# FFN of a hybrid decoder step: other edges between projection, row blocks and end, and split weights kept in memory

## The chip, the cores and the metric

One core of a Trainium2 chip runs the whole kernel. It has five engines with their own instruction queues, which run in order: TensorE (PE: matmuls; PEld is its load of the stationary operand), VectorE (DVE), ScalarE (ACT), GpSimd (POOL) and SyncE (SP), which here only issues DMAs. The metric is device microseconds of one execution, and the figure that is compared is a median over runs.

## The reference

The reference runs one decoder layer on 2048 prompt rows with 16 learned meta rows ahead of them, and on 8 samples of 4 rows. Two groups of heads (retention and gated DeltaNet) mix the normalised rows; then come an output projection, a residual with a layer norm, a SwiGLU feed-forward network and a second residual with a layer norm. The change touches what follows the mixers:

```python
hp = layer_norm(ALPHA * hp + mp, ln1_g[layer], ln1_b[layer])
...
def swiglu(h, w_gate_up, w_down):
    gu = h @ w_gate_up
    return (jax.nn.silu(gu[..., :D_FF]) * gu[..., D_FF:]) @ w_down
...
hp = layer_norm(ALPHA * hp + swiglu(hp, w_gate_up[layer], w_down[layer]), ln2_g[layer], ln2_b[layer])
```

The width is 1024 and D_FF is 2816, so the hidden width is 22 slices of 128. All is float32.

## The kernel before

The kernel has three stages: `attention`, `project` (output projection, first norm) and `ffn`. A framework places the semaphores and chooses each engine's order of instructions: it works through the program text by priority, earliest text first, with its own model of durations, so that later text fills what it takes for gaps. On the chip each engine then keeps that order. Memory is taken in pools that open and close like a stack; a tile in a new pool waits until what lay at its address is released.

**Precision.** A float32 operand is split into a high part (a cast on ACT, L311) and a low part (a subtraction on DVE or POOL, L318); a product is three matmuls (high by high, high by low, low by high), issued by `mm3` at L368. All matmuls of a product with 4 pieces of K make 12 matmuls.

**Projection.** `project` takes 17 tiles: 16 of 128 prompt rows and one of the 32 sample rows. For a tile it multiplies the mixed heads by `wout` (48 matmuls of 512 columns into two PSUM tiles `d`), adds the residual on DVE (L1199), runs `layer_norm` (statistics on DVE, an inverse square root in some ten dependent DVE instructions of one column at L263 to L270, scaling on ACT at L302, gain on DVE at L304, bias on POOL at L306), and stores the rows. Two tiles later `transposed` turns the rows round on PE (L1209), copies them (L1210), and for each pair of tiles `sums` makes four differences on POOL (L1222) and stores seven operands in DRAM (L1229).

**FFN.** Rows are worked through in three `BLOCKS` of pairs of tiles. Gate and up for a hidden slice f are done with a scheme of seven half-size products instead of eight (`gateup`: X, Y, Z, X, Y, W, Z), so that a product streams n columns: n is 384 for the blocks with three pairs of prompt tiles, and 272 for the one with two pairs and the sample rows. In the kernel before that one comes first. The stationary operands are sums and differences of pieces of gate and up: `weights` loads a slice of `gu` (L1274, 1 MB), forms S on POOL (L1288) and splits it (ACT, DVE). It does this for every f in every block, one slice ahead. The moving operands are the seven stored ones; `tokens` loads (L1394) and splits them at the start of a block. After every second f, `down` multiplies the hidden slices by `w_down` (512 columns into PSUM tiles `d`, 6 matmuls for a tile and half), one unit of work between two products, and DVE adds each result to the rows `y` (L1380). The last `down` of a block also norms each tile and stores it. `step` calls between products place this work: `units` are pieces of `down`, `ws` the preparation of the next weights.

**At the edges.** The pools of `ffn` open after those of `project` have closed. At the end of a block the last `down` with its norms runs between the first products of the next one. After the last f of the last block the units that are left run to the end.

## Time and profile before

| | us |
|---|---|
| median of 3 runs (3038.37 to 3047.83) | 3041.84 |
| the profiled execution's own time | 3041.72 |
| its span, first to last instruction | 3039.9 |
| PE busy | 2865.1 (94%) |
| DVE busy | 2184.7 (72%) |
| ACT busy | 1148.7 (38%) |
| POOL busy | 1039.0 (34%) |

Busy PE is not PE at its peak: matmuls overlap, and one that is counted as 0.39 us long can follow the one before it by 0.23 us. The table by stretches therefore is read by the number of matmuls in a stretch, times the distance from one to the next where nothing is in the way. A chain of waits is followed back from an instruction to what released it; a line "DVE dl L318" in it says which engine and which line of the kernel the time went to.

### The profile page before, as it was taken

How to read it: one execution, taken by the hardware profiler on the slowest of the kernel's cores; microseconds unless marked ns; L12 is line 12 of the kernel's file. 1: busy time of each engine (PE TensorE's matmuls, PEld its weight loads, DVE VectorE, ACT ScalarE, POOL GpSimd, SP SyncE). 2: the span in 40 equal slices, each digit the busy share in tenths (PEclk: the TensorE clock that was granted, in tenths of full speed). 3: DMA queues.
4: the chain of work that ended last, by engine and by line, in shares of the span. 5: the costliest groups of instructions: out<-in, count | busy, mean ns of one | idle time of the engine just before them, and what ended most of it. 6: DMA issues, size and time to landing. Idle time of an engine off the chain costs nothing.

```text
span 3039.9 us, 47059 instructions
## 1 busy us (share of the span) xinstructions
PE 2865.1 (94%) x17930; PEld 2550.1 (84%) x17930; DVE 2184.7 (72%) x4547; ACT 1148.7 (38%) x2571; POOL 1039.0 (34%) x927
## 2 busy tenths in 40 slices
PE   7999999999999999999869999899999989999995
PEld 6888888888888887978758889789999988999994
DVE  7777677766776676667677777886666688666667
ACT  2434444444444435432243333433333343233331
POOL 1222222221222131236545444453343335343332
PEclk9999999999999999999979999999999999999998
DMA  7544544443444333366542222431212244121211
GB/s 272 200 172 161 182 147 156 157 151 147 156 152 153 122 114 122 111 206 205 191 167 84 91 84 97 149 124 59 77 59 74 76 136 139 56 77 62 71 63 42
DMA packets 132274, 384.75 MB, mean 127 GB/s; under 512 B 18144, under 2 KB 53520, under 8 KB 115664
## 3 DMA queue, kind: packets, MB, share of 16 engines
q1 hardware_dynamic: 132048, 381.74, 36.0%
q8 instruction: 141, 2.31, 0.3%
q14 instruction: 85, 0.70, 0.1%
HBM read 294.14 MB, written 87.56 MB: 126 GB/s over the span
## 4 chain that ended last, share of the span: by engine, by line
PE 59%; DVE 21%; issue 6%; POOL 6%; ACT 4%; DMA 3%; SPq 0%; POOLq 0%; ACTq 0%; DVEq 0%
PE pj L368 18%; PE d L368 16%; PE Y L368 4%; PE X L368 4%; POOL S L1288 4%; PE Z L368 4%; PE W L368 3%; DVE dl L318 2%; DVE s34l L318 1%; ACT s34h L311 1%; DMA fr<-bd 1%; DVE cacc L822 1%; ACT junk L773 1%; DVE y L1380 1%; DVE lnst L286 1%
## 5 line engine op out<-in xcount | busy, mean ns | idle before, releaser
L368 PE MATMUL pj<-wh,xT 128*128 128x256 f32 (+2 forms) x2176 | 458.2, 294 | 8.4 <-ACT wh L311 4.2
L368 PE MATMUL pj<-xT,wh 128*128 128x512 f32 (+1 forms) x1280 | 379.8, 381 | 1.8 <-ACT cpre L806 1.1
L368 PEld LDWEIGHTS pj<-wh,xT 128*128 128x128 f32 (+1 forms) x2176 | 352.5, 187 | 13.1 <-ACT wh L311 4.4
L368 PE MATMUL pj<-wl,xT 128*128 128x256 f32 (+3 forms) x1088 | 309.8, 285 | 0.5 <-POOL wl L318 0.5
L368 PE MATMUL d<-dl,fh 128*128 128x512 f32 (+1 forms) x748 | 299.9, 401 | 9.2 <-DVE dl L318 8.6
L368 PE MATMUL d<-dh,fh 128*128 128x512 f32 (+1 forms) x748 | 294.0, 394 | 8.1 <-DVE y L1380 8.0
L368 PE MATMUL d<-dh,fl 128*128 128x512 f32 (+1 forms) x748 | 297.6, 398 | 2.1 <-POOL fl L318 2.1
L318 POOL TENSOR_TENSOR fl<-ta,fh 128x384 fp32r<-128x384 f32 (+1 forms) x66 | 70.9, 1074 | 642.7 <-ACT fh L311 642.7
L1288 POOL TENSOR_TENSOR S<-fr 128x512 f32<-128x512 f32 x132 | 209.8, 1607 | 168.9 <-DVE s34l L318 108.3
L1380 DVE TENSOR_TENSOR y<-y,d 128x512 f32<-128x512 f32 (+1 forms) x352 | 238.8, 680 | 31.4 <-PE d L368 31.2
L368 PEld LDWEIGHTS pj<-xT,wh 128*128 128x128 f32 x1280 | 211.9, 194 | 25.2 <-issue 3.4
L368 PE MATMUL pj<-xT,wl 128*128 128x512 f32 (+1 forms) x640 | 229.6, 359 | 0.0
L368 PEld LDWEIGHTS pj<-wl,xT 128*128 128x128 f32 (+1 forms) x1088 | 204.5, 188 | 0.9 <-POOL wl L318 0.8
L368 PEld LDWEIGHTS d<-dl,fh 128*128 128x128 f32 (+1 forms) x748 | 138.0, 184 | 40.3 <-DVE dl L318 22.3
L368 PEld LDWEIGHTS d<-dh,fl 128*128 128x128 f32 (+1 forms) x748 | 138.1, 185 | 35.5 <-POOL fl L318 2.6
L318 DVE TENSOR_TENSOR a11l<-fr,a11h 128x512 fp32r<-128x512 f32 x66 | 52.3, 792 | 158.1 <-ACT a11h L311 158.1
L368 PEld LDWEIGHTS d<-dh,fh 128*128 128x128 f32 (+1 forms) x748 | 137.9, 185 | 30.7 <-DVE y L1380 11.3
L311 ACT CAST a11h<-fr 128x512 fp32r<-128x512 f32 x66 | 41.0, 621 | 291.9 <-DMA fr<-gu 291.9
L368 PE MATMUL X<-b,a11h 128*128 128x384 f32 (+1 forms) x528 | 125.5, 322 | 18.1 <-ACT b L311 13.9
L822 DVE SCALAR_TENSOR_TENSOR cacc<-cpre,cw,cacc 128x512 f32<-128x512 f32 (+1 forms) x144 | 115.8, 805 | 32.0 <-ACT cacc L820 30.5
L368 PE MATMUL Y<-t,s34h 128*128 128x384 f32 (+1 forms) x528 | 128.8, 328 | 8.5 <-DVE u L1325 4.3
L368 PEld LDWEIGHTS pj<-xT,wl 128*128 128x128 f32 x640 | 122.7, 192 | 16.8 <-issue 0.8
(333 smaller groups left out, 7809.5 us busy)
## 6 DMA issues: line engine op xcount, KB each, us to landing
fr<-gu SPq DMA_DIRECT2D x132, 512.0 KB, 3.9
wh<-parts SPq DMA_DIRECT2D x45, 1024.0 KB, 5.0
wl<-parts SPq DMA_DIRECT2D x45, 1024.0 KB, 6.7
fr<-dn SPq DMA_DIRECT2D x66, 512.0 KB, 3.9
parts<-wh SPq DMA_DIRECT2D x15, 1024.0 KB, 5.3
parts<-wl SPq DMA_DIRECT2D x15, 1024.0 KB, 6.9
raw<-wret SPq DMA_DIRECT2D x16, 512.0 KB, 5.2
raw<-wgd SPq DMA_DIRECT2D x16, 512.0 KB, 7.1
```

Source lines behind the costliest of these rows:

```text
L286: i = nc.vector.bn_stats(out=st[:, o], in_=x)
L311: i = nc.scalar.copy(out=h, in_=src)
L318: i = (nc.vector if el == "dve" else nc.gpsimd).tensor_tensor(out=l, in0=src, in1=h.bitcast(F32), op=ALU.subtract)
L368: self.nc.tensor.matmul(out, lhsT=a(k), rhs=b(k), start=first and k == 0 and i == 0, stop=last and k == kn - 1 and i == 2, skip_group_chec ...
L773: nc.scalar.activation(out=junk, in_=p[:, j, :], func=AF.Square, accum_out=sq[:, a, t:t + 1])
L822: nc.vector.scalar_tensor_tensor(out=ac, in0=pre[:, i:i + N], scalar=w(i), in1=ac, op0=ALU.mult, op1=ALU.add)
L1288: op = lambda o, x, z, f: nc.gpsimd.tensor_tensor(out=o, in0=x, in1=z, op=f)
L1380: nc.vector.tensor_tensor(out=ys, in0=ys, in1=p, op=ALU.add)
```

## The change

The block with the sample rows becomes the last one. The pools for raw loads, gate/up weights, two of the seven token operands and the rows `y`, and all PSUM pools of the FFN, open before the projection; the projection's accumulators and transposes share the three PSUM tiles `d`, and its transposed rows and differences use the FFN's row tiles. The transposes of the last two projection tiles become units between the first FFN products. In block 1 each split weight is also stored in DRAM (`keep`, 2 x 14 KB a partition and slice); blocks 2 and 3 load it from there (`kept`) and neither load `gu` nor form S nor split. Norms at a block's end run for a group of tiles, one inverse square root for the group, in steps (`chores`). The middle `down` of a block goes through all tiles for one half of the columns and then for the other. In the last slice the order of products changes (`late`), half of its `down` runs before the last product, and `finish` does the other half: six PSUM tiles, to which the rows `y` are added by a matmul with the identity, normed from PSUM.

```diff
 BLOCKS = [
-    Block([(_P(0), _P(1), 128), (_P(2), _P(3), 128), (0, NS // 2, NS // 2)]),
...
+    Block([(_P(i), _P(i + 1), 128) for i in (0, 2, 4)]),
+    Block([(_P(i), _P(i + 1), 128) for i in (6, 8, 10)]),
+    Block([(_P(12), _P(13), 128), (_P(14), _P(15), 128), (0, NS // 2, NS // 2)]),
 ]
+LAID = (("a11", 0, 4), ("s12", 4, 8), ("a12", 12, 4), ("a22", 16, 4), ("s34", 20, 8))
...
+    def layer_norms(self, work, g, b, pool, sums=None):
...
+        for i, (x, rows) in enumerate(work):
...
+                nc.vector.bn_stats(out=st[:, o], in_=sums[i][o] if sums else x[:, 512 * o:512 * o + 512])
+            nc.vector.bn_aggr(out=mv[:rows, i], in_=st)
+            yield
+        r = self.rsqrt(mv[:, :, 1], T, 128, pool, 1.0, LN_EPS)
...
+        yield
...
+            if sums and i == T - 1:
+                for o, p in zip(at, src):
+                    nc.vector.scalar_tensor_tensor(out=x[:, o], in0=p, scalar=mv[:rows, i, 0:1], in1=g[:rows, o], op0=ALU.subtract, op1=ALU.mult)
+                for o in at:
+                    nc.vector.scalar_tensor_tensor(out=x[:, o], in0=x[:, o], scalar=r[:rows, i:i + 1], in1=b[:rows, o], op0=ALU.mult, op1=ALU.add)
...
+            for o, p in zip(at, src) if sums else [(slice(0, D), x)]:
+                nc.scalar.activation(out=x[:, o], in_=p, func=AF.Identity, scale=r[:rows, i:i + 1], bias=nm[:rows, i:i + 1])
+            nc.vector.tensor_tensor(out=x, in0=x, in1=g[:rows], op=ALU.mult)
+            for u, o in enumerate(at):
+                (nc.vector if sums and u else nc.gpsimd).tensor_tensor(out=x[:, o], in0=x[:, o], in1=b[:rows, o], op=ALU.add)
+            yield
...
+        spare = lambda i: self.fy.tile([128, D], F32, tag=f"y{i}", name="spare")
...
+            x = xr[r0] = spare(int(second)).rearrange("p (a b) -> p a b", a=8)
+            for j in range(2):
+                p = self.pd.tile([128, 512], F32, tag="d", name="tr").rearrange("p (a b) -> p a b", a=4)
...
+        def rest():
+            for i in (N - 2, N - 1):
+                yield from transposed(i)
...
-            pd = self.pool("p_d", bufs=3, space=PSUM, es=s)
-            pt = self.pool("p_t", bufs=3, space=PSUM, es=s)
...
+            ap, rp, sp, yp, pg, pd = self.fa, self.fr, self.fs, self.fy, self.pg, self.pd
...
+            def kept(f, w):
+
+                yield
+                for i, (name, o, m) in enumerate(LAID):
+                    t = [ap.tile([128, m, 128], F32R, tag=name + x, name=name + x, bufs=2 if name == "a11" else 1) for x in "hl"]
+                    for x, y in zip(t, self.wd[f]):
+                        nc.sync.dma_start(out=x.bitcast(F32).rearrange("p a b -> p (a b)"), in_=y[:, 128 * o:128 * (o + m)])
+                    w.update(named(name, t))
+                    yield
+                    if i in (0, 2):
+                        yield
...
+            def keep(f, name, t):
+                o, m = next((o, m) for n, o, m in LAID if n == name)
+                for x, y in zip(t, self.wd[f]):
+                    nc.sync.dma_start(out=y[:, 128 * o:128 * (o + m)], in_=x.bitcast(F32).rearrange("p a b -> p (a b)"))
+                return named(name, t)
...
-                t = parts(pair(2), "s34")
+                w.update(keep(f, "s34", parts(pair(2), "s34")))
...
+                if late:
+
+                    product(X, "a12", "b21", more=True)
+                    step(2)
+                    product(Y, "s3", "t3", more=True)
+                    add(u3, x1, Y)
+                    step(3)
+                    product(W, "a22", "t4")
+                    add(x1, u3, W)
+                    swish(X, x1, 0, "ta")
+                    step(4)
+                    product(Z, "s1", "t1")
+                    add(z5, u3, Z)
+                    add(u2, u2, Z)
+                    step(5)
+                    late(fh, fl)
+                    X = ps("X")
+                    product(X, "s4", "b22")
+                    add(u2, u2, X)
+                    swish(u2, z5, 1, "tb")
...
+            def normed(bi, group):
+
+                tiles, y = BLOCKS[bi].tiles(), rows_of[bi]
+                yield from self.layer_norms([(y[j][:tiles[j][1]], tiles[j][1]) for j in group], g2, b2, sm)
+                for j in group:
+                    nc.sync.dma_start(out=self.O["y"][tiles[j][0]:sum(tiles[j]), :], in_=y[j][:tiles[j][1]])
+                    if bi + 1 < len(BLOCKS) and j < len(BLOCKS[bi + 1].tiles()):
+                        load_rows(bi + 1, j)
...
+                order = [(n, i) for n in range(2) for group in groups for i in group]
+                if first or last:
+                    order = [(n, i) for group in groups for i in group for n in range(2)]
...
+            def finish(bi, fs, w, fi):
...
+                banks = [(pd, "d")] * 3 + [(pg, t) for t in "YWZ"]
...
+                        down1(blk, fs, w, fi, i, n, p, False)
+                        nc.tensor.matmul(p, lhsT=self.ident[:rows, :rows], rhs=y[i][:rows, 512 * n:512 * n + 512], start=False, stop=True)
...
+                for _ in self.layer_norms([(y[j][:tiles[j][1]], tiles[j][1]) for j in group], g2, b2, sm, sums):
+                    pass
...
+                    t = (self.fb if j < 2 else bp).tile([128, 2, 4 * 384], F32R, tag=name, name=name)
...
+                        self.split(r, h[:, o:o + m], l[:, o:o + m], "act", "pool" if u and bi else "dve")
...
+            units, chores = [rest], []
...
+                    ws = iter(()) if (bi, f) == end else weights(nf, nw) if bi == 0 and nf else kept(nf, nw)
...
+                        for _ in range(3 if (bi, f) == end else 1 if f % 2 or i >= (2 if bi + f else 4) else 0):
+                            some(units)
+                        for _ in range(2 if f == 2 else 1):
+                            some(chores)
+                        next(ws, None)
...
+                with self.weights_es:
+                    self.attention()
+                    self.fr = self.pool("f_r", bufs=4, es=late, side="right")
...
+                    self.pg = self.pool("p_g", space=PSUM, es=late)
+                    rest = self.project()
+                self.ffn(rest)
```

## Rows read from the trace of the kernel before

**Rows 1.** The page's head: the span, the busy time of each engine, and what the DMA engines moved in each of 40 equal slices of the span (76 us each), in GB/s.

```profile
span 3039.9 us, 47059 instructions
PE 2865.1 (94%) x17930; PEld 2550.1 (84%) x17930; DVE 2184.7 (72%) x4547; ACT 1148.7 (38%) x2571; POOL 1039.0 (34%) x927
GB/s 272 200 172 161 182 147 156 157 151 147 156 152 153 122 114 122 111 206 205 191 167 84 91 84 97 149 124 59 77 59 74 76 136 139 56 77 62 71 63 42
```

**Rows 2.** The FFN in seven stretches, all engines. Columns: stretch in us from the start, its length, busy us and (count of) instructions of PE, PEld, DVE, ACT, POOL, then PE's granted clock as a share of full speed, the DMA engines' busy share, and GB/s.

```profile
1505.60:1600.00 94.40, 57.39 (x339) 50.27 (x338) 67.90 (x86) 37.77 (x66) 49.31 (x36) 0.78 0.46 160
1600.00:1930.50 330.50, 329.92 (x2137) 295.57 (x2136) 252.48 (x373) 128.54 (x243) 158.14 (x130) 1.00 0.27 90
1930.50:2010.00 79.50, 64.71 (x316) 56.41 (x315) 77.72 (x139) 36.74 (x54) 38.60 (x27) 0.96 0.51 167
2010.00:2460.00 450.00, 447.99 (x2334) 414.13 (x2333) 302.33 (x418) 146.62 (x234) 166.08 (x117) 1.00 0.22 74
2460.00:2540.00 80.00, 67.58 (x309) 60.01 (x308) 78.51 (x146) 34.42 (x49) 40.27 (x27) 0.90 0.42 146
2540.00:2990.00 450.00, 447.70 (x2319) 412.39 (x2319) 303.74 (x420) 142.48 (x226) 162.29 (x113) 1.00 0.21 71
2990.00:3039.90 49.90, 17.37 (x71) 12.33 (x70) 41.20 (x115) 7.76 (x8) 14.88 (x12) 0.72 0.16 64
```

**Rows 3.** The same stretches, only the instructions that write or read the tile `d` of `down` (512 columns each); the first column after the length is PE, the third DVE.

```profile
1505.60:1600.00 94.40, 10.31 (x39) 6.18 (x39) 4.74 (x7) 0.78 0.46 160
1600.00:1930.50 330.50, 147.26 (x564) 91.54 (x562) 63.81 (x94) 1.00 0.27 90
1930.50:2010.00 79.50, 21.20 (x74) 13.44 (x74) 7.28 (x11) 0.96 0.51 167
2010.00:2460.00 450.00, 184.49 (x706) 130.02 (x706) 80.39 (x118) 1.00 0.22 74
2460.00:2540.00 80.00, 25.62 (x86) 17.84 (x86) 9.45 (x14) 0.90 0.42 146
2540.00:2990.00 450.00, 190.31 (x730) 134.46 (x730) 85.58 (x126) 1.00 0.21 71
2990.00:3039.90 49.90, 13.67 (x48) 8.63 (x48) 11.31 (x18) 0.72 0.16 64
```

**Rows 4.** The chain of waits in an undisturbed part of the second block: start us, us, what. A piece is as long as PE took from its first matmul to the next piece.

```profile
2108.80 2.08 PE X L368 x12
2110.88 1.39 PE d L368 x6
```

**Rows 5.** PE's instructions in order of time in an undisturbed part of the first block (start us, duration); twelve matmuls of product Y lie between these two starts.

```profile
1642.15 0.42 PE L368 MATMUL Y<-t,s34h 128*128 128x272 f32 x2
...
1643.66 0.39 PE L368 MATMUL d<-dh,fh 128*128 128x512 f32 x1
```

**Rows 6.** The chain of waits from the last projection matmul to the first products of the FFN (start us, us, what).

```profile
1505.83 0.70 DVE oy L1199
...
1515.54 1.27 POOL oy L306
...
1525.88 4.07 DMA fr<-gu
...
1540.07 1.50 PE X L368 x5
```

**Rows 7.** The projection, and the first 40 us after it, in the columns of rows 2.

```profile
1320.00:1505.60 185.60, 185.60 (x875) 150.54 (x874) 133.41 (x273) 48.02 (x59) 106.02 (x75) 1.00 0.63 196
1505.60:1546.00 40.40, 12.55 (x59) 10.36 (x58) 20.41 (x28) 13.58 (x21) 18.56 (x14) 0.58 0.52 183
```

**Rows 8.** DVE's instructions grouped by line and shape between 1930.5 and 2010 us: count | busy us, mean ns | idle before.

```profile
L270 DVE SCALAR_TENSOR_TENSOR rqy<-rqt,rqy 128x1 f32<-128x1 f32 x12 | 10.0, 830 | 0.0
L269 DVE SCALAR_TENSOR_TENSOR rqt<-rqy,rqa 128x1 f32<-128x1 f32 x12 | 8.3, 694 | 0.0
...
L318 DVE TENSOR_TENSOR s12l<-S,s12h 128x1024 fp32r<-128x1024 f32 x3 | 3.7, 1248 | 0.0
...
L318 DVE TENSOR_TENSOR t<-fr,t 128x512 fp32r<-128x512 f32 x4 | 3.3, 819 | 0.0
...
L1325 DVE TENSOR_TENSOR u<-x,Y 128x384 f32<-128x384 f32 x5 | 2.6, 530 | 0.0
```

**Rows 9.** DVE and POOL in order of time, at the end of the kernel (start us, duration).

```profile
3027.84 2.48 POOL L306 TENSOR_TENSOR y<-y,b 128x512 f32<-128x512 f32 x2 [3.43 <-DVE rqy L270]
3027.87 2.46 DVE L269 SCALAR_TENSOR_TENSOR rqt<-rqy,rqa 128x1 f32<-128x1 f32 x2
...
3030.56 0.22 DVE L269 SCALAR_TENSOR_TENSOR rqt<-rqy,rqa 128x1 f32<-128x1 f32 x1
...
3033.43 2.92 POOL L306 TENSOR_TENSOR y<-y,b 128x512 f32<-128x512 f32 x2 [3.11 <-DVE y L304]
```

**Rows 10.** DMA issues: what, count, KB each, median us from issue to landing. `parts` is where the attention stage keeps its own split weights in DRAM.

```profile
wl<-parts SPq DMA_DIRECT2D x45, 1024.0 KB, 6.7
...
parts<-wl SPq DMA_DIRECT2D x15, 1024.0 KB, 6.9
```

**Rows 11.** PE in order of time in the attention stage: four matmuls of unsplit float32 operands with 512 columns, and the next start.

```profile
259.79 1.98 PE L674 MATMUL pj<-ub,rkd 32*128 32x512 f32 x4
261.70 0.52 PE L368 MATMUL pj<-xT,wh 128*128 128x280 f32 x2
```

More of the change, by code (lines that the diff above doesn't have):

```diff
@@ L1240, in project, with ffn @@
             g1, b1 = self.vec_bcast(2, vp, "g1"), self.vec_bcast(3, vp, "b1")
-            N = len(work)
-            for i in range(N + 2):
-                if i < N:
-                    project(i)
-                    if i and i + 1 < N:
-                        load(i + 1)
+            for i in range(N):
+                project(i)
+                if i and i + 1 < N:
+                    load(i + 1)
                 if i >= 2:
-                    transposed(i - 2)
-    def ffn(self):
+                    for _ in transposed(i - 2):
+                        pass
+        return rest()
+    def ffn(self, rest):
         nc, I = self.nc, self.I
@@ new lines, in grouped, with down1 @@
+                firsts = [i for i, (r0, rows) in enumerate(tiles) if r0 in [p[0] for p in blk.pairs] and rows == 128]
+                return firsts, [i for i in range(len(tiles)) if i not in firsts]
+            def down1(blk, fs, w, fi, i, n, p, last=True):
+                self.mm3(p, lambda f: blk.columns(fs[f][0], i), lambda f: blk.columns(fs[f][1], i),
+                         lambda f: w[n][0][:, fi[f]], lambda f: w[n][1][:, fi[f]], len(fs), True, last)
+            def normed(bi, group):
[5 more added lines that the diff above has]
+                        load_rows(bi + 1, j)
@@ new lines, in load_rows, with down @@
+            def load_rows(bi, i):
+                r0, rows = BLOCKS[bi].tiles()[i]
+                rows_of[bi][i] = yp.tile([128, D], F32, tag=f"y{i}", name=f"y{i}")
+                o = BLOCKS[bi].row(r0)
+                nc.sync.dma_start(out=rows_of[bi][i][:rows], in_=self.yd[bi][o:o + rows, :])
+            def down(bi, fs, w, fi, first, last, groups=None):
+                blk, y = BLOCKS[bi], rows_of[bi]
+                tiles = blk.tiles()
+                groups = groups or grouped(blk)
+                order = [(n, i) for n in range(2) for group in groups for i in group]
+                if first or last:
+                    order = [(n, i) for group in groups for i in group for n in range(2)]
+                for n, i in order:
+                    rows = tiles[i][1]
+                    p = pd.tile([128, 512], F32, tag="d", name="d")[:rows]
+                    down1(blk, fs, w, fi, i, n, p)
+                    ys = y[i][:rows, 512 * n:512 * n + 512]
+                    if first:
+                        nc.vector.scalar_tensor_tensor(out=ys, in0=ys, scalar=ALPHA, in1=p, op0=ALU.mult, op1=ALU.add)
+                    else:
+                        nc.vector.tensor_tensor(out=ys, in0=ys, in1=p, op=ALU.add)
+                    for group in groups:
+                        if last and n and i == group[-1]:
+                            chores.append(normed(bi, group))
+                    yield
@@ L1425, in ffn @@
                     w = nw
[L1426 to L1429 removed]
+                    if (bi, f) == (0, 1):
+                        for i in range(len(blk.tiles())):
+                            load_rows(0, i)
                     g = f // 2
[L1431 to L1434 removed]
+                    if (bi, f) == end:
+                        while chores:
+                            some(chores)
+                        finish(bi, fs, dw, [1])
+                    elif (bi, g) == (end[0], ng - 1):
+                        dw = downw(g)
+                        units.append(down(bi, fs, dw, [0], False, False))
                         fs = []
                     elif f % 2:
[L1437 removed]
+                        units.append(down(bi, fs, downw(g), [0, 1], g == 0, g == ng - 1))
                         fs = []
[L1439 to L1441 removed]
     def mix_pos(self, r0):
@@ L1461, in build @@
             self.bd, self.yd = {}, []
+            self.wd = [[self.dr.tile([128, 28 * 128], F32, tag=f"wd{f}{x}", name="wd") for x in "hl"] for f in range(NF)]
             for bi, blk in enumerate(BLOCKS):
```

209 lines of the change are left out of this document (105 added, 104 removed).

## The prediction

> **What bounds the kernel now.** I read the page's head first, then the FFN by stretches, then chains and timelines at the places where the stretches differ. TensorE is busy for 94% of the span [rows 1], but busy says little here, so I count matmuls. Where nothing is in the way, twelve matmuls of 384 columns take 2.08 us and six of 512 take 1.39 us [rows 4], so 0.173 and 0.232 us each; of 272 columns twelve take 1643.66 - 1642.15 = 1.51 us, 0.126 each [rows 5]. Per stretch, the `d` matmuls of [rows 3] cost 0.232, the rest of [rows 2] the product's pitch, and what the stretch is longer than that is lost:
>
> - 1505.6 to 1600 (**first edge**): 39 x 0.232 + 276 x 0.126 = 43.7 (339 - 39, less 24 transposes), lost 50.7 with the transposes.
> - 1600 to 1930.5: 564 and 1573 of 272 columns, 328.6, lost 1.9.
> - 1930.5 to 2010 (**second edge**): 74 and 242 of 384, 59.1, lost 20.4.
> - 2010 to 2460: 706 and 1628, 445.7, lost 4.3.
> - 2460 to 2540 (**third edge**): 86 and 223, 58.6, lost 21.4.
> - 2540 to 2990: 730 and 1589, 444.5, lost 5.5.
> - 2990 to the end: 48 and 23, 15.1, lost 34.8.
>
> In all 139 us, of which 127 lie at four edges; the middles run at PE's pitch. The reader is to see in these rows that DVE is the engine in the way at the two inner edges (77.7 of 79.5 and 78.5 of 80 us busy) and that at the first one no engine is full: it is a chain [rows 6] from the last projection matmul over its norm (POOL's bias at 1515.5), the transposes and differences to the load of `gu` at 1525.9, which stands behind the stores on SP's queue, and then to products from 1540 on. In the first 40 us PE was granted a 0.58 share of its clock [rows 7], that is, it spent most of them at 1.2 GHz.
>
> **The change part by part.** The matmul work stays: two blocks of 384 and one of 272 columns either way. So the middles cost the same, and the sum is of the edges.
>
> *First edge, now 50.7.* Raw loads, weights of slice 0 and the operands b11 and t2 have memory of their own during the projection, in which DVE is busy for 133, POOL for 106 and ACT for 48 of 185.6 us [rows 7], so they are ready at its end, and X and Y can start at once. The last tile's norm, its transposes and `sums` leave the path, as they now belong to the third block. What is late next: the five other operands lie where the projection's weights were, so their splits start only at the end of the projection. On DVE a split is 1.25 + 0.82 us [rows 8], 10.3 for five; the last norm is some 6 of the 9.7 us between 1505.83 and 1515.54 [rows 6]; six additions and four gate steps at 0.53 make 5.3; the weights of slice 1 make 2 x 1.25 + 3 x 0.82 = 5.0. That is 26.6 us against 84 x 0.173 = 14.6 of products and some 2.6 of transposes: 9.4 late. With 4 us for the first operand to come and the 2.6 of transposes I take 16 as the new loss. Bounds: 5 (all splits in time) and 35 (the order again puts a chain in front).
>
> *Projection.* Accumulators and transposes now share three PSUM tiles. The next tile's first matmul needs the bank that L1199 is just reading: 0.70 us [rows 6] against eight transposes, estimated at 0.11 each (just under the 0.126 of 272 columns [rows 5]), 0.9. With DVE busy for 72% [rows 7] the read can come late by a quarter of a microsecond; x 16 tiles I take 4. Bounds: 0, and 16 x 1.25 = 20, were a gain or subtraction always just ahead of it.
>
> *Second and third edge, now 20.4 and 21.4.* From the 77.7 us of DVE in the second, three slices of weight splits go (15), the shorter splits of tokens go to POOL (4 x 0.82 and as much again for b, some 5), and of the 18.3 us of L269 and L270 at least half (two inverse square roots for a block in place of one per tile). That leaves some 49 us for 59 of matmuls: DVE is no longer full. Late next are the operands: loaded, cast and split one after another, each only when the product that read the old one is done. I take 6 each; bounds 0 and 20.
>
> *Middles, now 11.7.* Going through all tiles for one half of the columns frees half of the `w_down` weights earlier; I take 10, bounds 5 and what the second rival makes.
>
> *Added traffic.* A slice's split weights are 2 x 28 x 128 x 128 x 4 B = 3.67 MB. In block 1 they are written beside 1.05 MB of `gu` and 0.52 MB of `w_down` per 22.9 us (7 x 2.08 + 6 x 1.39): 229 GB/s. Block 2 reads 4.2 MB per 22.9 us (183), block 3 per 17.6 us (7 x 1.51 + 5 x 1.39: 239), where 71 to 90 were moved [rows 2]. The attention stage and the projection move 111 to 272 [rows 1] with such pieces landing in 6.7 and 6.9 us [rows 10]. The tightest piece, s34 (1 MB, one buffer), can be issued when the last product of a slice is done and is needed by the fifth of the next: 4 x 1.51 + 3 x 1.39 = 10.2 us in block 3, 12.5 in block 2. So I cost it at nothing; the four products and three units before it are its cover. SP's queue holds rows, `w_down` and outputs behind such a load's wait, but that wait ends with a product that PE reaches in any case.
>
> *End, now 34.8.* From the last product on, six steps of about 0.53 (addition, gate, split) make 3.2. Then six PSUM tiles, each 3 x 0.232 and one float32 matmul with the identity. The nearest row has four of those with 512 columns in 1.91 us [rows 11], 0.48 each: 6 x 1.18 = 7.1. (At half clock 14; I take full.) Statistics of the last half about 0.9; thirteen one-column DVE steps at 0.22 [rows 9] make 2.9; then DVE's share of three tiles: two times a gain (1.25) and half a bias (0.8), and four passes of 0.8, 7.3. From POOL's last instruction to the end of the span it was 3039.9 - 3036.35 = 3.5 [rows 9]. Together 24.9, less 18 x 0.232 of old matmul work: 21 lost. Bounds 15 and 33.
>
> One rule of the skill speaks against the norms as they are put. In the rows, two L269 of one column took 2.46 us while POOL added biases, and 0.22 when it did not [rows 9]. The Trainium skill (SBUF — State Buffer, "Who interferes with whom") has it that a DVE instruction with two SBUF inputs and a POOL instruction that reads SBUF shut each other out for their whole length; the trace agrees. By that rule the splits that go to POOL would hold DVE up at the inner edges, where I leave it slack, and POOL's two half biases of 1.25 would add some 2.5 us at the end; by the rows alone, with POOL idle in the inverse square root, the end stays as above.
>
> **Sum.** Lost after: 16 + 4 + 6 + 6 + 10 + 21 = 63, before 139: 76 us less. The profiled execution took 3041.7 us (the span and 1.8 around it), within 0.2 of the median shown. Forecast: **2965 us**.
>
> **The rivals.**
>
> *The edges stay ordered badly.* The engines keep an order that a model chose. If the last projection norm and the weights of slice 1 stand ahead of the token splits, and the norm steps ahead of what PE waits for, the first edge loses 32, the inner ones 14 each, the end 30, and 4 + 11 as above: 105, a gain of 34, **3008 us**. For it: the present order already loses 20 at edges where PE's work would cover DVE's. Against it: DVE is relieved by a third.
>
> *The kept weights come late.* If s34 takes 14 us to land under three times the traffic, each slice of block 3 waits 3.8 us and each of block 2 1.5: 22 x 5.3 = 117, against a gain of 76: **3083 us**, slower than before. It decides from a landing of about 13 us: with 22 x (2.8 + 0.5) = 73 the gain is gone. For it: SP's queue is in order, and a late piece delays all that follow. Against it: 6.7 us at up to 272 GB/s.
>
> *The edges all but close.* Splits in time and no half clock: 7 + 0 + 3 + 3 + 6 + 16 = 35 lost, 104 gained, **2938 us**. For it: the engines other than PE are under three quarters busy in the middles [rows 2]. Against it: 26.6 us of DVE work against 17 at the first edge.
>
> *The change does not do what it says*, as the early pools get no memory before the projection ends: then the first edge stays at 50 and the rest comes, 3000 us; it falls in with the first rival.
>
> **How the numbers follow.** Forecast 0.60, edges ordered badly 0.22 (with the last), weights late 0.08, edges all but close 0.10. The forecast's own range is 2948 to 2990, from the bounds of the first edge and the end. For 8 in 10 I go to 2930 below, which takes in the third case, and to 3010 above. No change that this kernel's measurement can tell is within 0.3%, 9 us: 3033 to 3051. Faster takes all but the late weights and the tail of the first rival: 0.89; same 0.04; slower 0.07.
>
> **What would show it.** In the profile after: X and Y of the first slice directly behind the last projection matmul, and no stretch at half clock there; DVE under 85% at the inner edges, with no `s12l` or `s34l` in blocks 2 and 3; no PE wait on a weight load there, and a landing of `s34` below 10 us; the last matmul some 15 us before the end. PE waiting in the middles of blocks 2 and 3 for a DMA, or a first product over 15 us after the projection, would make the prediction wrong.

## The result, and the profile after

The changed kernel takes 2996.3 us, median of 4 runs (2993.9 to 2997.8), against 3042.8 of the kernel before on the same chip (median of 4): a ratio of 0.9846, 95% interval 0.9834 to 0.9858. The forecast was 2965 with a range of 2930 to 3010. So 46.5 us came of the 76 that the sum gave. The profiled execution took 2997.0 us and has a span of 2995.2.

The head of the page after, to set beside [rows 1]:

```profile
span 2995.2 us, 47489 instructions
...
PE 2864.0 (96%) x17942; PEld 2554.5 (85%) x17942; DVE 1932.5 (65%) x4203; ACT 998.9 (33%) x2352; POOL 783.7 (26%) x761
...
GB/s 259 203 171 154 200 122 152 148 170 153 150 157 154 135 121 122 125 166 232 216 196 289 249 222 229 227 231 266 271 182 187 176 183 183 272 292 239 243 226 86
```

DVE lost 252 us of work and POOL 255, and from slice 21 to the last but one DMA moves 176 to 292 GB/s, where the middles of the FFN moved 71 to 90 [rows 2]. The twelve extra PE instructions are the identity matmuls of `finish`.

Busy time of the engines by stretches (columns: stretch, its length, then busy us and count of PE, PEld, DVE, ACT and POOL, granted clock, DMA share, GB/s), and in a second fence, for the first and the last stretch of the FFN, the same, without POOL, for the instructions on the tiles `d` alone:

```profile
1303.80:1528.80 225.00, 209.28 (x960) 164.87 (x959) 161.34 (x313) 66.55 (x93) 119.79 (x81) 0.99 0.64 206
1528.80:1613.00 84.20, 62.23 (x299) 56.45 (x298) 51.28 (x69) 31.94 (x51) 36.67 (x29) 0.86 0.78 263
1613.00:2050.00 437.00, 437.00 (x2277) 406.37 (x2277) 298.42 (x396) 145.39 (x229) 170.06 (x112) 1.00 0.68 238
2050.00:2110.00 60.00, 60.00 (x316) 56.15 (x315) 50.04 (x93) 20.64 (x32) 23.31 (x16) 1.00 0.81 291
2110.00:2540.00 430.00, 430.00 (x2242) 400.06 (x2241) 195.84 (x306) 79.23 (x137) 52.14 (x45) 1.00 0.58 192
2540.00:2640.00 100.00, 96.16 (x583) 87.04 (x582) 75.16 (x135) 31.19 (x55) 38.02 (x31) 0.98 0.80 284
2640.00:2960.00 320.00, 320.00 (x2066) 286.47 (x2065) 161.62 (x282) 63.02 (x142) 35.61 (x55) 1.00 0.67 226
2960.00:2995.20 35.20, 15.94 (x50) 8.78 (x48) 24.76 (x60) 6.10 (x9) 9.48 (x6) 0.72 0.17 64
```

```profile
1528.80:1613.00 84.20, 7.91 (x24) 5.74 (x23) 2.04 (x3) 0.00 (x0) 0.86 0.78 263
2960.00:2995.20 35.20, 9.45 (x23) 5.38 (x21) 4.62 (x7) 2.12 (x3) 0.72 0.17 64
```

Counted with the pitches of the prediction, and with the work that the kernel before had (1395.3 us of FFN matmuls), the losses are:

| | before | forecast | after | how |
|---|---|---|---|---|
| projection, longer by | 0 | 4 | 23 | 225.0 against 202 |
| first edge | 50.7 | 16 | 35 | 84.2 less 251 x 0.173 and 24 x 0.232 |
| inner edges and middles | 53.5 | 22 | 8 | 1347 less 1338.8 (the 1395.3 without the first edge's 49.0 and the end's 7.5) |
| end | 34.8 | 21 | 28 | 35.2 less 12 x 0.126 and 26 x 0.232 |
| sum | 139 | 63 | 94 | |

That is 45 us less, as the spans say (3039.9 - 2995.2). The reader is to see that the block of 1347 us in the middle, in which PE is busy to the last hundredth in four of five rows, did better than forecast, and that three other places did worse. What PE waited for tells where; first from 1330 to 1528 (projection), then from 1528 to 1613 (first edge), then from 1613 to 2960:

```profile
PE d L406 <- DVE oy L1273: 8.5, 8, 2.9
...
PE d L406 <- ACT dh L349: 7.0, 1, 7.0
PE tr L1217 <- POOL spare L309: 6.4, 1, 6.4
PE X L406 <- ACT a11h L349: 1.8, 1, 1.8
PE X L406 <- DVE a11l L356: 1.7, 1, 1.7
...
PE d L406 <- DVE y L1493: 3.2, 1, 3.2
PE Y L406 <- DMA s34l<-wd: 0.6, 1, 0.6
```

In the projection PE waits for L1273, the addition that empties an accumulator: the sharing of three tiles `d`. At the first edge it waits for the first `w_down` (`dh` is its high part), for the last tile's norm (`spare`) and for split weights. In the 1347 us behind it, it waits 3.8 us in all, and 0.6 for a kept weight.

### The profile page after: what moved, and what is told of

It is laid out like the page before. It is cut to its first block, busy times and chain, and to the rows that moved or that the text cites. A ratio compares the mean times of both kernels' runs of the same rounds, so it can differ in the third digit from the quotient of the medians.

```text
span 2995.2 us, 47489 instructions
## 1 busy us (share of the span) xinstructions
PE 2864.0 (96%) x17942; PEld 2554.5 (85%) x17942; DVE 1932.5 (65%) x4203; ACT 998.9 (33%) x2352; POOL 783.7 (26%) x761
## 4 chain that ended last, share of the span: by engine, by line
PE 77%; DVE 13%; DMA 3%; ACT 3%; issue 3%; POOL 1%; SPq 1%; POOLq 0%; ACTq 0%; DVEq 0%
PE d L406 20%; PE pj L406 19%; PE Z L406 8%; PE X L406 8%; PE Y L406 8%; PE W L406 4%; ACT junk L811 1%; DVE cacc L860 1%; PE w L978 1%; PE w L971 1%; PE pj L712 1%; PE w L980 1%; PE rt L666 1%; DVE wl L356 1%; DMA fr<-gu 1%
## 5 line engine op out<-in xcount | busy, mean ns | idle before, releaser
L406 PEld LDWEIGHTS pj<-wh,xT 128*128 128x128 f32 (+1 forms) x2176 | 354.5, 189 | 11.8 <-ACT wh L349 3.3
L356 POOL TENSOR_TENSOR fl<-ta,fh 128x384 fp32r<-128x384 f32 (+1 forms) x65 | 63.2, 972 | 768.3 <-issue 542.4
L406 PEld LDWEIGHTS pj<-xT,wl 128*128 128x128 f32 x640 | 122.9, 192 | 16.8 <-issue 0.8
L860 DVE SCALAR_TENSOR_TENSOR cacc<-cpre,cw,cacc 128x512 f32<-128x512 f32 (+1 forms) x144 | 115.8, 804 | 32.4 <-ACT cacc L858 30.9
L1394 DVE TENSOR_TENSOR u<-x,Y 128x384 f32<-128x384 f32 (+1 forms) x132 | 67.5, 511 | 100.7 <-PE Y L406 97.8
L961 POOL TENSOR_TENSOR Lm<-LT,lvl 128x512 f16<-128x512 f32 (+1 forms) x108 | 129.2, 1228 | 11.3 <-DVE LT L949 10.5
L349 ACT CAST fh<-ta 128x384 fp32r<-128x384 f32 (+1 forms) x66 | 31.8, 482 | 287.7 <-DVE ta L1402 287.7
L406 PE MATMUL X<-b,a12h 128*128 128x384 f32 (+1 forms) x528 | 126.1, 325 | 0.0
```

The source lines that it names most:

```text
L349: i = nc.scalar.copy(out=h, in_=src)
L356: i = (nc.vector if el == "dve" else nc.gpsimd).tensor_tensor(out=l, in0=src, in1=h.bitcast(F32), op=ALU.subtract)
L406: self.nc.tensor.matmul(out, lhsT=a(k), rhs=b(k), start=first and k == 0 and i == 0, stop=last and k == kn - 1 and i == 2, skip_group_chec ...
L860: nc.vector.scalar_tensor_tensor(out=ac, in0=pre[:, i:i + N], scalar=w(i), in1=ac, op0=ALU.mult, op1=ALU.add)
L961: nc.gpsimd.tensor_tensor(out=Lm[:, x - 1], in0=LT, in1=lvl(x), op=ALU.mult)
L1394: add = lambda o, x, p: nc.vector.tensor_tensor(out=o, in0=x, in1=p, op=ALU.add)
```

## The experiments

Each run was timed beside the kernel before on the same chip, so the ratios can be compared; the changed kernel itself, run again among them (e8), is the measure.

| run | us | ratio to before, 95% interval |
|---|---|---|
| e8, the changed kernel again | 2996.2 | 0.9847 (0.9832 to 0.9862) |
| e1, own banks for transposes | 2982.3 | 0.9804 (0.9791 to 0.9818) |
| e2, mixed heads in the FFN's ring | 3014.2 | 0.9906 (0.9892 to 0.9919) |
| e3, late transposes | 2993.0 | 0.9837 (0.9824 to 0.9851) |
| e4, first `w_down` ahead of rows | 2993.1 | 0.9838 (0.9825 to 0.9852) |
| e5, weights split again | 3025.9 | 0.9946 (0.9933 to 0.9960) |
| e6, identity first | 2993.2 | 0.9836 (0.9818 to 0.9854) |
| e7, e1 + e2 + e3 + e4 + e6 | 3000.8 | 0.9861 (0.9844 to 0.9878) |
| e9, stores issued by ScalarE | 2983.9 | 0.9803 (0.9790 to 0.9817) |
| e10, first mixed heads in row buffers | 2995.1 | 0.9839 (0.9826 to 0.9852) |
| e11, e1 + e4 + e6 + e10 | 2970.1 | 0.9763 (0.9749 to 0.9776) |
| e12, e11 + e9 | 2971.1 | 0.9761 (0.9748 to 0.9775) |

> The changed kernel itself, unchanged, beside the others of this call, as their measure: 2994 to 2998 us, a ratio to the kernel before of 0.984 to 0.986.

It came out so, at 2996.2.

### The projection: shared banks, shared ring

```diff
-                p = self.pd.tile([128, 512], F32, tag="d", name="tr").rearrange("p (a b) -> p a b", a=4)
+                pool, tag = (self.pd, "d") if i >= N - 2 else (self.pg, "WZ"[j])
+                p = pool.tile([128, 512], F32, tag=tag, name="tr").rearrange("p (a b) -> p a b", a=4)
```

> The transposes of the first fifteen projection tiles use two PSUM banks of the FFN's products that are idle then, in place of the three that the accumulators use. Theory A (the shared banks make the projection wait at each tile boundary): the projection falls from 225 us by 8 to 14, the halves behind a boundary go back from 6.4 to 9.4 us to about 6.3, the time falls to 2983 to 2988 us. Rival B (DVE is late at the boundaries in itself, by its order, and the bank only shows it): the projection falls by 3 us at most, the time stays at 2993 to 2997.

The time fell by 14 us. The projection by stretch, e1:

```profile
1302.80:1513.80 211.00, 205.22 (x958) 164.42 (x958) 161.75 (x313) 65.71 (x93) 119.41 (x81) 0.99 0.68 220
```

It is 14 us shorter (211.0 against 225.0) with the same 161 us of DVE work in it, and from 1330 on there is no PE wait left. From the third on a tile takes 11.7 to 11.9 us in e1 and 11.7 to 12.0 in the kernel before, against 12.0 to 14.9 in the changed one (the last tile, of 32 rows, takes some 11 in all three). Theory A holds: DVE is not late in itself; what comes late is the tile `d`, which the transposes take too.

The other 9 us lie in the first two tiles (22.5 and 12.6 us; before 15.2 and 10.9).

```diff
-                raw = self.raw.tile([128, 4, 256], F32, tag="raw", name="raw").rearrange("p a b -> p (a b)").rearrange("p (a b) -> p a b", a=8)[:, :, :rows]
+                raw = self.fr.tile([128, 4, 256], F32, tag="fr", name="fr").rearrange("p a b -> p (a b)").rearrange("p (a b) -> p a b", a=8)[:, :, :rows]
```

> The loads of the mixed heads in the projection use the FFN's ring of four raw buffers, so they no longer queue for the two buffers that the loads of wout go through. Theory A (the common ring makes the start of the projection wait): the first three halves take 20 to 23 us together in place of 29.7, the time falls by 6 to 9 us, to 2987 to 2990. Rival B (the start is bound by loading and splitting wout, and the mixed heads are only last by chance): the first three halves stay above 27 us, the time falls by less than 3.

Neither: 18 us slower. SyncE's issues in e2 (start, length, what, count):

```profile
1300.56 6.54 SPq L378 DMA_DIRECT2D raw<-wout  x3
...
1309.21 0.33 SPq L378 DMA_DIRECT2D raw<-wout  x1
1312.75 2.69 SPq L697 DMA_DIRECT2D mixd<-mx  x4
1316.74 3.95 SPq L1257 DMA_DIRECT2D fr<-mixd  x4
```

The last load of `wout` is now issued at 1309.2, where it was at 1318.4 after the change and at 1309.8 before it; so much of theory A is right, and the first two tiles take 14.5 and 10.9 us as in the kernel before. But they start later, with more of the loads already done, so the price of the ring can't be read from them. The first mixed heads, issued at 1291.3 in the changed kernel, stand here behind the last stores of the attention stage, at 1316.7, and the projection starts at 1322.1 in place of 1303.8. Why they are put there (memory of that ring that comes free late, or the framework's model) was not tried. e10 asks the same question with buffers that are free:

```diff
-                raw = self.raw.tile([128, 4, 256], F32, tag="raw", name="raw").rearrange("p a b -> p (a b)").rearrange("p (a b) -> p a b", a=8)[:, :, :rows]
+                raw = yp.tile([128, D], F32, tag="oy", name="oy") if i < 2 else self.raw.tile([128, 4, 256], F32, tag="raw", name="raw").rearrange("p a b -> p (a b)")
+                raw = raw.rearrange("p (a b) -> p a b", a=8)[:, :, :rows]
```

> Only the first two loads of mixed heads leave the ring of two raw buffers and go to the two buffers of projection rows that are free at that time; the loads of wout keep the ring to themselves, as in the kernel before. Theory A (the common ring delays the last loads of wout by some 8 us): they are issued by about 1311 in place of 1318, the first three halves take 20 to 23 us in place of 29.7, the time falls by 6 to 9 us, to 2987 to 2990. Rival B (DVE's and POOL's splits set the pace of the loads in any case): above 27 us, under 3 us of gain.

The last `wout` load goes out at 1314.7, and the first two tiles take 17.3 and 11.7 us, 6.1 less than in the changed kernel: theory A by the place, rival B by the time, which fell by 1 us only. The gain is given back at the next boundaries: the third tile takes 18.5 us in place of 14.9, and PE's waits for L1274 (the addition of before, one line on) rise from 8.5 to 9.7 us with 2.9 more before a transpose. With banks of their own (e11) the first two tiles take 16.8 and 11.5, and the projection 207.1 us, 3.9 less than with the banks alone, where e10 alone gives 0.9 (224.1 against 225.0). So one loss hid behind the other.

### The first edge: who stands in whose queue

```diff
-                        for _ in range(3 if (bi, f) == end else 1 if f % 2 or i >= (2 if bi + f else 4) else 0):
+                        for _ in range(3 if (bi, f) == end else 1 if f % 2 or i >= (2 if bi + f else 7) else 0):
                             some(units)
```

> The transposes and differences of the last projection tiles become units of the second slice alone, no longer of the end of the first. Theory A (PE's order holds the transposes of the sample tile ahead of a norm that is not done): the wait of 6.4 us on the sample tile's rows goes, and with it some of the half clock behind it: 6 to 10 us less, 2986 to 2990. Rival B (another chain is as late behind it: the down weights, or the norm itself): under 2 us, and the wait moves to a dh or an a operand of the second slice.

A miss of the experiment: the edit moved the text and not the work. The wait of 6.4 us is still there, at the same place between the third and the fourth product. The framework set the transposes there again, though the text has them a slice later; what it took for a gap of PE stands in no trace. The waits of 1.8 and 1.7 us on `a11` are gone and that on `dh` is 10.7 us in place of 7.0; the 3 us in the medians are less than the intervals tell apart. Why the transposes wait is in DVE's and POOL's rows of the changed kernel (start, length, what; in brackets idle time and releaser):

```profile
1530.54 1.20 DVE L356 TENSOR_TENSOR t<-fr,t 128x1024 fp32r<-128x1024 f32 x1
...
1532.93 1.20 DVE L356 TENSOR_TENSOR b<-fr,b 128x1024 fp32r<-128x1024 f32 x1
...
1538.69 1.21 DVE L307 TENSOR_TENSOR spare<-spare,g 32x1024 f32<-32x1024 f32 x1
1539.83 2.41 DVE L356 TENSOR_TENSOR t<-fr,t 128x512 fp32r<-128x512 f32 x3
1526.52 2.53 POOL L309 TENSOR_TENSOR spare<-spare,b 128x512 f32<-128x512 f32 x2 [3.02 <-DVE spare L307]
1539.98 4.61 POOL L309 TENSOR_TENSOR spare<-spare,b 32x512 f32<-32x512 f32 x2 [10.93 <-DVE spare L307]
```

The norm of the sample tile is woven into the token splits (L356) from 1530 to 1540, and its two biases on POOL take 4.6 us (the first 3.4, the second, with DVE done, 1.3), where the tile before took 2.5 for both.

```diff
                     if (bi, f) == (0, 1):
+                        dw = downw(0)
                         for i in range(len(blk.tiles())):
                             load_rows(0, i)
...
-                        units.append(down(bi, fs, downw(g), [0, 1], g == 0, g == ng - 1))
+                        units.append(down(bi, fs, dw if (bi, f) == (0, 1) else downw(g), [0, 1], g == 0, g == ng - 1))
```

> The first load of w_down stands ahead of the loads of the rows y in the text, so ahead of them on SP's queue. Theory A (the first down waits because its weights are queued behind row loads that wait for the projection's stores): the wait of 7.0 us on dh goes, 5 to 8 us less, 2988 to 2991. Rival B (the rows take the place: the addition to y, and with it the PSUM bank, comes late by as much): under 2 us, with a wait on DVE's L1493 or on the row load in place of dh.

By the trace the wait on `dh` falls from 7.0 to 2.2 us and the FFN's stretch to 2075 loses 32.7 us in place of 36.7. In the medians it is 3 us, less than the intervals tell apart. So theory A by the wait, but not by its price of 5 to 8 us.

e5 (below) leaves the stores of the split weights out. Over the first 545 us of the FFN it lost 13 us less, and 17.6 less by the end of this edge: 545 us on, e5 is already in its second edge. That led to e9, which only moves their issue:

```diff
                 for x, y in zip(t, self.wd[f]):
-                    nc.sync.dma_start(out=y[:, 128 * o:128 * (o + m)], in_=x.bitcast(F32).rearrange("p a b -> p (a b)"))
+                    nc.scalar.dma_start(out=y[:, 128 * o:128 * (o + m)], in_=x.bitcast(F32).rearrange("p a b -> p (a b)"))
```

> The stores of the split weights in block 1 are issued by ScalarE in place of SyncE; nothing else changes. With the stores left out the first 545 us of the FFN lost 23.7 us in place of 36.7. Theory A (the stores stand in SP's one queue, and what is queued behind them, row loads and w_down, comes late): the first edge loses 24 to 30, the time falls by 6 to 12, to 2984 to 2990. Rival B (the stores themselves cost: they hold the single buffers of the weights, or share the DMA engines with the loads): the loss stays at 34 to 38 and the time within 4 us of 2996. Rival C (a DMA issue that waits for DVE's low part holds ScalarE up): 5 us slower or more.

Theory A: 12 us less in the medians. By the traces this edge is 7.6 us shorter (29.1 lost to 2075 in place of 36.7). What SyncE itself waited for from 1528 to 1613 in the changed kernel (L1344 is the store):

```profile
SPq L1344 <- ACT a11h L349: 9.3, 3, 5.3
...
SPq L1344 <- DVE a11l L356: 4.3, 3, 1.9
SPq L1344 <- DVE s12l L356: 3.1, 2, 2.4
...
SPq L1344 <- DVE a12l L356: 2.1, 1, 2.1
```

A store waits for the split that it stores, in these four rows for 18.8 us, and everything behind it in SyncE's queue waits with it: row loads, `w_down`, the next `gu`. In e9 PE's waits at this edge on `dh` and on `a11` are 0.8 us in place of 10.5:

```profile
PE tr L1217 <- POOL spare L309: 6.4, 1, 6.4
PE W L406 <- ACT a22h L349: 2.9, 1, 2.9
PE Y L406 <- ACT s12h L349: 2.4, 1, 2.4
...
PE d L406 <- ACT dh L349: 0.8, 1, 0.8
```

Some 2 us of that come back in the waits for W and Y (2.9 and 2.4 in place of 1.6 and 1.5). Their casts now share ACT with the issues, and ACT waits 2.3 us for the low part `s12l` ahead of the cast of `a22h`: a little of rival C. And e5 stays 10 us ahead of e9 at this edge. Whether that is the stores' bytes (311 GB/s here in e9, 184 in e5), the single buffers that they hold (rival B) or ACT's queue, no run tells apart.

### The inner edges: is it the kept weights?

```diff
-                for x, y in zip(t, self.wd[f]):
-                    nc.sync.dma_start(out=y[:, 128 * o:128 * (o + m)], in_=x.bitcast(F32).rearrange("p a b -> p (a b)"))
...
-                    ws = iter(()) if (bi, f) == end else weights(nf, nw) if bi == 0 and nf else kept(nf, nw)
+                    ws = iter(()) if (bi, f) == end else weights(nf, nw)
```

> Undoes one part: the weights of blocks 2 and 3 are loaded from gu, summed and split again, and nothing is kept in memory; all else is as in the changed kernel. Theory A (the inner edges close because the kept weights take DVE's load off, as the prediction's sum has it: some 15 us of DVE work in each edge): the edges at 2050 to 2110 and 2540 to 2640 lose 5 to 12 us each, DVE is again above 90% busy there, the time rises by 10 to 25 us, to 3006 to 3021. Rival B (the norms in steps close the inner edges alone, and the kept weights are worth nothing, or cost with their 3.67 MB a slice): within 4 us of the changed kernel's 2996, on either side.

30 us slower, more than theory A asked. Two inner edges and the stretch behind them, e5, and in a second fence its PE waits from 2040 to 2980:

```profile
2050.00:2110.00 60.00, 53.25 (x257) 47.69 (x256) 53.86 (x91) 22.66 (x34) 35.67 (x24) 0.94 0.45 152
2540.00:2640.00 100.00, 87.76 (x499) 78.39 (x498) 86.70 (x138) 42.30 (x70) 55.49 (x41) 0.93 0.42 130
2640.00:2980.00 340.00, 326.47 (x2084) 289.41 (x2083) 261.36 (x373) 126.85 (x236) 155.96 (x132) 0.98 0.27 89
```

```profile
PE d L406 <- DVE y L1491: 13.8, 2, 11.0
PE Z L406 <- DVE u L1392: 11.1, 7, 5.1
```

DVE is busy for 90% and 87% of these two stretches, where the changed kernel has 83% and 75%, and the longest waits are on DVE. (e5 comes to the second edge 18 us earlier; from 2032 to 2092 DVE is 89% busy in it.) Both kernels issue the matmuls of the FFN in the same order, so they can be compared matmul by matmul, here by the start in us behind the start of the projection's last matmul, transposes not counted:

| FFN matmul | changed | e5 | e5 later by |
|---|---|---|---|
| 400th, behind the first edge | 108.7 | 91.1 | -17.6 |
| 2600th, ahead of the second | 530.4 | 512.8 | -17.6 |
| 3000th, behind it | 607.4 | 610.0 | 2.6 |
| 5200th, ahead of the third | 1029.4 | 1032.0 | 2.6 |
| 5800th, behind it | 1128.6 | 1159.7 | 31.1 |
| 7799th, the last | 1449.8 | 1483.7 | 33.9 |

So keeping the weights costs 17.6 us at the first edge and nothing in the rest of block 1, and is worth 51.5 us behind it: 20 at the second edge, 28.5 at the third, 3 in the last block. Without it the rest of the change is worth 16 us (3042.0 to 3025.9). At the inner edges and in the middles e5 loses some 60 us (8 and 51.5), no less than the 53.5 of the kernel before: by themselves the norms in steps, the token splits on POOL and the new order of `down` close nothing there in e5, and rival B falls. The other parts of the change (the order of the blocks, the early pools, `finish`) were not undone one by one; what they gain is read from before and after alone.

### The end

```diff
...
-                        down1(blk, fs, w, fi, i, n, p, False)
-                        nc.tensor.matmul(p, lhsT=self.ident[:rows, :rows], rhs=y[i][:rows, 512 * n:512 * n + 512], start=False, stop=True)
+                        nc.tensor.matmul(p, lhsT=self.ident[:rows, :rows], rhs=y[i][:rows, 512 * n:512 * n + 512], start=True, stop=False)
...
+                for i, s in zip(group, sums):
+                    for n, p in enumerate(s):
+                        down1(blk, fs, w, fi, i, n, p, False)
```

> In the end part the identity matmuls that add the rows come first in each PSUM tile, while the gate of the last product is still being formed, and the six matmuls of each tile follow. Theory A (the gap of 3.2 us for the gate is free for the six identity matmuls of 0.45 us, and without the gap PE keeps its full clock): the last matmul ends 5 to 8 us earlier, the time falls to 2988 to 2991. Rival B (the clock falls all the same, or the rows are not ready): 0 to 3 us less.

PE's rows at the last product's end, first of the changed kernel, then of e6:

```profile
2963.02 0.29 PE L406 MATMUL X<-b,s34l 128*128 128x272 f32 x1
2966.52 0.79 PE L406 MATMUL d<-dh,fh 128*128 128x512 f32 x1 [3.21 <-ACT fh L349]
...
2968.39 1.91 PE L1515 MATMUL d<-y,ident 128*128 128x512 f32 x2
...
2976.33 1.04 PE L1515 MATMUL W<-y,ident 32*32 32x512 f32 x2
```

```profile
2965.47 0.29 PE L406 MATMUL X<-b,s34l 128*128 128x272 f32 x1
2965.59 2.74 PE L1514 MATMUL d<-y,ident 128*128 128x512 f32 x6
...
2970.95 0.50 PE L406 MATMUL d<-dh,fh 128*128 128x512 f32 x1
...
2974.99 0.40 PE L406 MATMUL Z<-dh,fl 128*32 128x512 f32 x1
```

From the last product's last matmul to the last of all it is 15.6 us in the changed kernel (2978.57 - 2963.02) and 9.5 in e6, the 6 us that theory A gave, and the half clock in between is gone: granted 0.77 from 2966.5 to 2979 in the changed kernel, 1.00 from 2965 to 2976 in e6. From that last product to the end of the span only 3 of the 6 are left (28.9 us against 32.2), and 3 in the median, inside the intervals: in e6 DVE still does the two gains of the first group (2.34 us from 2973.26, as in the changed kernel) ahead of the last statistics, and two instructions of the inverse square root take 0.79 and 0.64 us beside POOL where they take 0.39 and 0.15 in the changed kernel. The bound passes from PE to DVE.

### Together

> Five edits together: own banks for the transposes, the mixed heads in the other ring, the late transposes only in the second slice, the first w_down load ahead of the rows, the identity matmuls first. If the five losses are separate, their gains add up: 25 to 38 us less than the changed kernel, 2958 to 2971. If the first edge is bound by one chain behind another (rows, norm, token splits), its two edits gain only what the longer one gives, and the sum is 12 to 22 us: 2974 to 2984.

It has e2's late start in it (projection from 1327.9 on), so the sum can't be read from the total. Its projection takes 208.1 us. Its first edge, from the projection to 2084, still loses 38 us: the gains of e3 and e4 alone do not add up there.

> Four edits together: own banks for the transposes (measured alone: 14 us less), the first two loads of mixed heads in the buffers of rows, the first w_down load ahead of the rows, and the identity matmuls first (each of the last two alone: some 3 us less). If they add up: 2996 - 14 - 7 - 3 - 3 = 2969, between 2965 and 2974. If the first edge is bound by the norm of the last tile whatever comes before it, or the wout loads gain nothing: 2975 to 2982.

2970.1, as added up: 26 us faster than the changed kernel and 73 than the one before (ratio 0.9763). By the traces the projection is 17.9 us shorter and the FFN behind it 6.4 (3.7 at the first edge). This version beats both.

> The four edits of the run before and the stores of the split weights issued by ScalarE. With the stores alone the FFN's stretch to 2075 lost 29.1 in place of 36.7 us, with the four edits 33.0. If the stores' queue is still what the four edits leave at the first edge: 4 to 8 us less than the 2970 of the four, 2961 to 2967. If the first w_down load ahead of the rows had already taken that gain: within 3 us of 2970.

2971.1: no gain over e11 in the medians; by the traces the first edge loses 30.9 us in place of 33.0. What e9 gains alone and what e4 gains alone are in good part the same wait on `dh`, and with it gone the wait of 6.2 us on the sample tile's norm stays, with 4.9 on the cast of `a22h`.

## Why the prediction was right or wrong

**Projection, +4 forecast, +23 measured.** The step named the place and the price of one boundary, but took DVE's read as late by a quarter of a microsecond. e1 puts 14 us on the 16 boundaries, 0.9 each, inside the bound of 20 that the text gave. The other 9 us were not in the sum at all: the mixed heads' own ring of buffers went, and the loads of `wout` now share two buffers with them. It stands in the change, and the sum had no term for it. By the first two tiles e10 and e11 show 6 to 7 of the 9 to be this ring; the rest is open.

**First edge, 16 forecast, 35 measured.** X and Y start right behind the projection (the first X at 1529.8, behind eight transposes), as said, and the early pools do what they were to do. What failed is the step that late operands would be the only loss, worked out as DVE work against PE work. The chain in front, bound 35 in the text, came: 6.4 us on the sample tile's norm, which the step had taken off the path as work of the third block. Its transposes serve the third block, but the framework set them between the products of block 1's first slice, and e3 could not move them. And "I cost it at nothing" failed for the stores: their price was looked for in GB/s. Leaving them out wins 17.6 us at this edge (e5); moving only their issue off SyncE's queue wins 7.6 there by the trace and 12 in the medians (e9). So the order of SyncE's queue is a good part of the price, and the rest is open. PE waited 21.9 us in all here. The stretch at the lower clock, which was to be gone, is there too: at a granted clock of 0.86 over 84.2 us, at most 11.8 more went to it, and the transposes took some 2.

**Inner edges and middles, 22 forecast, 8 measured.** The mechanism was right in its main part: DVE is relieved by the kept weights, and e5 shows it by undoing them. What the step counted beside them, 14 of the 29 us off DVE by norms in steps and by splits on POOL, closes nothing alone in e5. The mis-sized term is the operands, taken as 6 us late at each edge: at the second none was, at the third one row load (3.2 us). The 10 us for the middles were too many as well. DVE had 50 us of work in the 60 of the second edge, as the step had it (49). The loads of kept weights cost nothing, as forecast: 0.6 us of waits, pieces of 512 KB landing in 3.7 to 5.6 us in the median, and 291 GB/s beside PE at its full pace (316 matmuls from 2050 to 2110, 59.9 us at the prediction's pitches). The fastest and the slowest of these pieces, from 2110 to 2560 and from 2640 to 2960 (what, count, KB each, median us from issue to landing):

```profile
s34h<-wd SPq DMA_DIRECT2D x19, 512.0 KB, 3.7
...
s34l<-wd SPq DMA_DIRECT2D x17, 512.0 KB, 5.6
```

The rival of late weights (3083 us; its gain gone from 13 us of landing on) fell.

**End, 21 forecast, 28 measured.** Gate 3.5 us (3.2 said); PE 12.1 to its last matmul (7.1 said); statistics 1.6 (0.9); inverse square root 3.7 (2.9); the rest of the norms 7.6 (7.3); tail 3.7 (3.5). The mis-sized term is PE's. A float32 matmul with the identity appears as two instructions, and the step counted one of 0.48 for each. The four instructions of [rows 11] are two matmuls, a loop of two in the program, so the row itself said 0.95. In e6, where nothing disturbs them, three take 2.74 us, 0.9 each, so six cost 5.4 and not 2.9. The rest, some 2.5 us, goes with the half clock (granted 0.77) after the gate's gap of 3.2 us, which the text had named ("At half clock 14; I take full").

The rule of the Trainium skill that was weighed there (SBUF — State Buffer, "Who interferes with whom") shows in both places. The rows of DVE's last two gains and of POOL's bias beside the second:

```profile
2985.52 1.23 DVE L341 TENSOR_TENSOR y<-y,g 128x1024 f32<-128x1024 f32 x1 [0.26 <-ACT y L340]
...
2987.39 2.28 DVE L341 TENSOR_TENSOR y<-y,g 128x1024 f32<-128x1024 f32 x1
...
2986.82 1.77 POOL L343 TENSOR_TENSOR y<-y,b 128x512 f32<-128x512 f32 x1 [6.32 <-DVE y L341]
```

At the end the second gain takes 2.28 us beside POOL's bias, where the one before took 1.23: 1 us of the 2.5 that the prediction weighed, and the norms came out near the rows' sum. At the first edge, where I had not applied it, POOL's bias stood 3.4 us in place of 1.3 beside DVE's splits, and that was on PE's path.

So the likeliest case held by its sign and by what the kept weights do. That the time stayed within 2930 to 3010 is in part luck, as misses of both signs met: three places lost 45 us more than forecast (19, 19 and 7) and the inner edges and middles 14 less. The first edge (35) and the end (28) came near the first rival's 32 and 30, the projection beyond any case, and the inner edges and middles (8) beyond the third rival's 12. The forecast's own range (2948 to 2990) was missed by 6 us. It does not follow from its bounds at the upper end: 35 at the first edge and 33 at the end are 31 us above the forecast, 2996.

## What to carry to other kernels

A transfer is priced by its bytes and by its place: a store that waits for a result holds up every load behind it on the same queue, so give it another queue or put urgent loads ahead of it; here either alone took the wait on `dh` from 7.0 us to 0.8 or 2.2, and both together (e12) gained no more in time. When pools or PSUM tiles are merged, list each ring that disappears and who else now takes its buffers; here 14 us stood in the shared tiles `d` and most of another 9 in the ring that went. And measure small gains in company: one loss can hide behind another (the ring behind the banks), and two edits can remove the same wait (stores and `w_down`). A part that is meant to help should also be undone alone: here only that showed that the kept weights carry all of the gain at the inner edges, and what their stores cost.

## What was not expected of the hardware

- A plain float32 matmul of 512 columns with the identity takes two instructions of 0.45 us, 0.9 in all (e6, granted clock 1.00), where one of the split kind takes 0.23.
- Loads at 291 GB/s beside PE at its full pace took nothing from it that can be measured: 316 matmuls in 60 us, 59.9 at the pitches of the quiet stretches, granted clock 1.00.
- An instruction of DVE on three columns is held up beside POOL too: L267 took 0.64 us beside POOL's bias in e6, and 0.15 behind it in the changed kernel.
